# Low weight parts made by ScalarE's negation and an accumulating DMA in place of a subtraction

## The chip, the core and the metric

The kernel runs on one core of a Trainium2 chip. Its metric is the device time of one execution in microseconds (us). Five engines work side by side, each through its own queue in program order: TensorE (PE: matmuls; PEld: weight loads), VectorE (DVE), ScalarE (ACT), GpSimd (POOL) and SyncE (SP, which here only issues DMAs). Waits between engines are semaphores that the framework puts in from the data each instruction reads and writes.

## What is computed

One step of a four-layer decoder trunk over 512 prompt rows and 32 sample rows of width 1024. Each layer is a token mixer and a SwiGLU network, and the layers have a different mixer each: pooling, a Conformer convolution, a chunked gated MLP, a short convolution.

```python
for i in range(DEPTH):                       # 4 layers
    h = _rmsnorm(x, norm_mix[i])
    y, s = mixer[i](h, ...)                  # pool, conv, chunk_gmlp, short_conv
    x = x + y
    x = x + _swiglu(_rmsnorm(x, norm_ffn[i]), ffn_w_in[i], ffn_w_out[i])

def _swiglu(h, w_in, w_out):                 # D_FF = 2816
    gate, up = jnp.split(jnp.einsum('bld,df->blf', h, w_in), 2, axis=-1)
    return jnp.einsum('blf,fd->bld', jax.nn.silu(gate) * up, w_out)
```

All is float32, and nearly all the arithmetic is in the products with the weights.

## The kernel before

**Three matmuls a product.** TensorE takes its operands in a rounded form of float32 (F32R). To keep the precision, every weight and every activation is split into a high part (the value rounded to F32R) and a low part (the value less the high part), and a product is high x high + high x low + low x high, three matmuls into one accumulator. For a weight the high part is a cast on ScalarE (`Load.high`, L159), and the low part a subtraction raw - high (`Load.low`, from L161) on VectorE or GpSimd. All operations of VectorE, GpSimd and TensorE are recorded at L102, the helper that keeps an estimate of each engine's time (`dve.t`, `pool.t`, `pe.t`).

**Loads.** A weight load is 128 partitions by 1024, 768 or 640 columns: `raw_fi`, `hi_fi`, `lo_fi` and so on. The letters say which product it belongs to: fi and fo are the input and output product of the SwiGLU networks, ci and co of the convolution layer, gi and go of the gated layer, si, sb and so of the short convolution. The raw part is fetched by SyncE's queue (L155). There are four raw buffers, five high buffers (AHI + 1) and four low buffers (ALO + 1).

**Halves.** The 544 rows are two halves: A (256 columns) and B (256 + 32). Up to the second layer's network the two halves go through the layers in turn ("one-half" steps), so that each weight is loaded twice; the convolution's taps for one half, a long row of VectorE operations, run as a background job beside the other half's products. From the gated layer's input product on, both halves are worked in one step ("joint"), except for the gated layer's output product, which is done for A and then for B. A one-half step with a 1024-column load is 24 matmuls, a joint one 48. A step of an output product (fo) takes two loads, 768 and 640 columns, and is 33 or 66 matmuls.

**Order of the work.** The program is a list of steps (`Stream`). `Stream.run` goes through it once, and for each step calls `fetch`, which emits the casts up to four loads ahead of the step's first one, and the low parts up to three ahead; then the step's matmuls; then the evacuations of the step before (on VectorE and ScalarE); then background work, as long as `dve.t` is less than a due time that is worked out from `pe.t`. So a load's cast stands on ScalarE's queue ahead of the evacuations of the step before it was fetched. A buffer's next user waits until TensorE has done the step that last read it.

**Who subtracts.** `share` decides. Where it is true (the networks and products with `rel=True`, that is layer 0's network for B, layer 1's for A, the convolution's input product, and the output products for A of the convolution and the gated layer), the subtraction goes to GpSimd unless `pool.t` runs more than LO_LAG ahead of `pe.t`; elsewhere to VectorE. GpSimd has no other large work in those stages, and hardly any later.

Of the kernel before, what the change touches and what calls it, by code (L numbers as in the profile page):

```python
# [8 lines left out]
F32 = mybir.dt.float32  # L9
F32R = mybir.dt.float32r  # L10
I32 = mybir.dt.int32
AF = mybir.ActivationFunctionType
ALU = mybir.AluOpType
PSUM = bass.MemoryType.PSUM

P = 128
# [48 lines left out]
def trunk_kernel(  # L65
# [7 lines left out]
    nc = tc.nc  # L73
# [4 lines left out]
    wp = ctx.enter_context(tc.tile_pool(name="wp", bufs=1))  # L78
# [3 lines left out]
    act = nc.scalar  # L82

    class Timed:
# [3 lines left out]
        def __init__(self, eng, size, per, fixed, least=0.0):  # L88
            self.eng, self.size, self.per, self.fixed, self.t = eng, size, per, fixed, 0.0
            self.least = least  # L90
# [57 lines left out]
    class Load:  # L148
        def __init__(self, src, n, name, share=0):
            self.src, self.n, self.name, self.share = src, n, name, share  # L150
            self.raw = self.hi = self.lo = None

        def dma(self):
            self.raw = wp.tile([P, 1024], F32, tag="raw", name=f"raw_{self.name}", bufs=NRAW)[:, : self.n]
            nc.sync.dma_start(self.raw, self.src)  # L155
# [4 lines left out]

        def low(self):  # L161
            n, raw = self.n, self.raw
            if self.share is True:
                k = 0 if pool.t < pe.t + LO_LAG else n
            else:
                s = (dve.t - pool.t - BIAS + n * dve.per) / (dve.per + pool.per) if self.share else 0
                k = n - min(max(int(s) // 32 * 32, 0), self.share)
            self.lo = wp.tile([P, 1024], F32R, tag="lo", name=f"lo_{self.name}", bufs=ALO + 1)[:, :n]
            if k:
                dve.tensor_sub(self.lo[:, :k], raw[:, :k], self.hi[:, :k].bitcast(F32))  # L170
            if k < n:
                pool.tensor_sub(self.lo[:, k:], raw[:, k:], self.hi[:, k:].bitcast(F32))
# [6 lines left out]
    class Stream:  # L179
        def __init__(self):  # L180
            self.steps, self.loads = [], []
            self.nd = self.nh = self.nl = 0
            self.pending, self.side, self.jobs, self.draining = [], [], [], False
            self.held, self.fill = False, None

        def add(self, loads, mm, evac, flush=False, fill=None):

            for l in loads:
                if l not in self.loads[-6:]:
                    self.loads.append(l)  # L190
            self.steps.append(Step(loads, mm, evac, flush, fill))

        def do(self, fn):
# [85 lines left out]
    S = Stream()  # L279
# [757 lines left out]


    gk = {}

    def gm_consts():
        k = cp.tile([P, PM_COLS], F32, tag="consts", name="gk")
        ws = k[:, :512].rearrange("p (g t) -> p g t", g=NG)
        bs = k[:, 512:1024].rearrange("p (g t) -> p g t", g=NG)
        wss = k[:NS, 1024:1152].rearrange("p (g t) -> p g t", g=NG)
        nc.sync.dma_start(ws, wsT)
        nc.sync.dma_start(wss, wsS)
        nc.sync.dma_start(bs, gm_bs.partition_broadcast(P))

        for g in range(NG):  # L1050
            for w_, n in ((ws, CH), (wss, NS)):
                pool.affine_select(
                    out=w_[:, g, :], in_=w_[:, g, :], pattern=[[1, n]],
                    compare_op=ALU.is_ge, fill=0.0, base=0, channel_multiplier=-1,
                )
        gk.update(ws=ws, bs=bs, wss=wss)
        for nm, src in (("g", gm_g), ("b", gm_b)):
            gk["ln" + nm] = []
            for g in range(NG):
                t = T(f"ln{nm}{g}")  # L1060
                nc.sync.dma_start(t[:, :256], q4(src)[g].partition_broadcast(P)[:, 0, :])
                gk["ln" + nm].append(t)
# [251 lines left out]
    S.run()  # L1314


NRAW, AHI, ALO = 4, 4, 3
FIRST = (
    ("W", (0,)), ("x", (0, 1)), ("w", (0,)), ("W", (1,)), ("x", (2, 3, 4, 5)), ("w", (1,)), ("lo", (0,)),
    ("x", (6, 7)), ("lo", (1, 2, 3, 4, 5, 6, 7)), ("W", (2,)), ("w", (2,)),  # L1320
# [131 lines left out]
```

## Time and profile before

| | |
|---|---|
| median of three runs | 2192.82 us (2192.27 to 2196.62) |
| profiled execution: time, span | 2191.2 us, 2189.3 us |
| TensorE busy | 2156.0 us (98%) |
| VectorE, ScalarE, GpSimd busy | 1298.7, 851.4, 542.7 us |
| moved by SyncE's queue | 279.47 MB in 110376 packets, 42.7% of 16 DMA engines |

"Busy" counts an engine's own instructions, not waiting or issuing. The table of stages in the prediction has, for a stretch of the span, each engine's busy time with its count of instructions in brackets, the clock that was granted to TensorE (1.00 is full), the busy share of the 16 DMA engines and what they moved. A row of waits names who waited, for whom, how many us in total, how often, and the longest. A row of a group has its count, then its busy time and the mean length of one in ns, then the engine's idle time ahead of it and what ended it. A row of DMA issues has the count, the KB of one and the median us from issue to landing. In a row of the timeline stand the start, the length, the engine, the operation, and in brackets the idle time ahead of it.

### The profile page before, as it was taken

Reading aid. Unit: us, or ns where it says so; the run is one execution under the profiler, and the core shown is the slowest. Engines: PE = TensorE matmul, PEld = TensorE weight load, DVE = VectorE, ACT = ScalarE, POOL = GpSimd, SP = SyncE. Lnnn points to the kernel's source line nnn. Section 1 sums busy time; section 2 is a strip of 40 time slices with the busy share of each in tenths; the row PEclk is TensorE's granted clock in tenths of the full one; section 3 lists DMA queues with packets and bytes.
Section 4 is the critical chain, followed back from the end, with each engine's and each line's share of the span. In section 5 each row is a group of like instructions: output and inputs, shape, how many; then the busy total and the mean of one; then the engine's idle time right before and its main releaser. Section 6 shows DMA issues by size and latency. Waiting matters only on the chain.

```text
span 2189.3 us, 41838 instructions
## 1 busy us (share of the span) xinstructions
PE 2156.0 (98%) x17110; PEld 2147.0 (98%) x17110; DVE 1298.7 (59%) x2613; ACT 851.4 (39%) x1372; POOL 542.7 (25%) x378
## 2 busy tenths in 40 slices
PE   9999999999999999999989999999999999999997
PEld 9999999999999999999989999999999999999997
DVE  7867798517999566565587443344555554434444
ACT  5445543545444654444335322232412233222332
POOL 3011787888788910000050000000000000000001
PEclk9999999999999999999999999999999999999998
DMA  8645555556755554545224223322345422232221
GB/s 272 196 144 167 180 183 154 173 160 183 172 164 179 170 191 142 187 146 174 79 91 140 88 70 95 106 85 67 111 81 89 97 87 88 63 102 96 81 74 61
DMA packets 112039, 284.07 MB, mean 130 GB/s; under 512 B 30540, under 2 KB 37800, under 8 KB 111584
## 3 DMA queue, kind: packets, MB, share of 16 engines
q1 hardware_dynamic: 110376, 279.47, 42.7%
q8 instruction: 134, 2.20, 0.4%
q10 hardware_dynamic: 1152, 1.32, 0.2%
q0 software_dynamic: 320, 0.62, 0.1%
q14 instruction: 57, 0.47, 0.1%
HBM read 277.11 MB, written 4.62 MB: 129 GB/s over the span
## 4 chain that ended last, share of the span: by engine, by line
PE 83%; DVE 12%; DMA 2%; ACT 1%; issue 1%; POOL 1%; SPq 0%; DVEq 0%; POOLq 0%; ACTq 0%
PE ps_o L102 22%; PE ps_g L102 20%; PE ps_u L102 20%; DVE ct L102 4%; PE ps_gv L102 3%; PE ps_co L102 2%; PE ps_sc L102 2%; PE ps_sx L102 2%; PE ps_sbg L102 2%; PE ps_so L102 2%; DVE cw L102 1%; DMA raw_fi<-in_w_fin 1%; PE ps_go L102 1%; PE ps_cg L102 1%; DVE vT L102 1%
## 5 line engine op out<-in xcount | busy, mean ns | idle before, releaser
L102 DVE TENSOR_TENSOR lo_fi<-raw_fi,hi_fi 128x1024 fp32r<-128x1024 f32 (+1 forms) x180 | 222.4, 1237 | 332.2 <-issue 258.2
L159 ACT CAST hi_fi<-raw_fi 128x1024 fp32r<-128x1024 f32 x264 | 276.4, 1049 | 346.5 <-PE ps_g L102 111.6
L102 PE MATMUL ps_o<-H_p,hi_fo 128*128 128x288 f32 (+1 forms) x1408 | 351.6, 288 | 1.2 <-ACT H_p L512 1.0
L102 PE MATMUL ps_o<-L_p,hi_fo 128*128 128x288 f32 (+1 forms) x1408 | 351.6, 288 | 0.2
L102 PE MATMUL ps_o<-H_p,lo_fo 128*128 128x288 f32 (+1 forms) x1408 | 351.3, 288 | 0.0
L159 ACT CAST hi_fo<-raw_fo 128x768 fp32r<-128x768 f32 x192 | 149.9, 782 | 287.1 <-PE ps_o L102 154.2
L102 PEld LDWEIGHTS ps_o<-H_p,hi_fo 128*128 128x128 f32 x1408 | 246.4, 188 | 1.6 <-ACT H_p L512 1.6
L102 DVE TENSOR_TENSOR lo_fo<-raw_fo,hi_fo 128x768 fp32r<-128x768 f32 (+1 forms) x128 | 113.5, 890 | 225.4 <-issue 104.8
L102 PEld LDWEIGHTS ps_o<-L_p,hi_fo 128*128 128x128 f32 x1408 | 246.4, 188 | 0.5 <-DVE L_p L102 0.5
L102 PEld LDWEIGHTS ps_o<-H_p,lo_fo 128*128 128x128 f32 x1408 | 246.7, 188 | 0.1
L102 PE MATMUL ps_g<-hH_f,lo_fi 128*128 128x256 f32 (+1 forms) x1040 | 241.8, 288 | 0.8 <-DVE lo_fi L102 0.8
L102 PE MATMUL ps_g<-hH_f,hi_fi 128*128 128x256 f32 (+1 forms) x1040 | 242.2, 288 | 0.1
L102 PE MATMUL ps_u<-hH_f,hi_fi 128*128 128x256 f32 (+1 forms) x1040 | 242.2, 288 | 0.0
L102 PE MATMUL ps_g<-hL_f,hi_fi 128*128 128x256 f32 (+1 forms) x1040 | 241.9, 288 | 0.0
L102 PE MATMUL ps_u<-hL_f,hi_fi 128*128 128x256 f32 (+1 forms) x1040 | 241.8, 287 | 0.0
L102 PE MATMUL ps_u<-hH_f,lo_fi 128*128 128x256 f32 (+1 forms) x1040 | 241.7, 288 | 0.0
L102 POOL TENSOR_TENSOR lo_fi<-raw_fi,hi_fi 128x1024 fp32r<-128x1024 f32 (+1 forms) x86 | 207.6, 2430 | 23.1 <-PE ps_g L102 6.9
L102 DVE SCALAR_TENSOR_TENSOR ct<-ce,colsT,ct 128x256 f32<-128x256 f32 x448 | 182.1, 480 | 0.0
L102 PEld LDWEIGHTS ps_g<-hH_f,lo_fi 128*128 128x128 f32 x1040 | 175.7, 188 | 1.0 <-DVE lo_fi L102 1.0
L102 PEld LDWEIGHTS ps_g<-hH_f,hi_fi 128*128 128x128 f32 x1040 | 176.1, 188 | 0.5 <-ACT hi_fi L159 0.3
L102 PEld LDWEIGHTS ps_u<-hH_f,hi_fi 128*128 128x128 f32 x1040 | 176.0, 188 | 0.1
L102 PEld LDWEIGHTS ps_g<-hL_f,hi_fi 128*128 128x128 f32 x1040 | 175.9, 188 | 0.0
(370 smaller groups left out, 4835.4 us busy)
## 6 DMA issues: line engine op xcount, KB each, us to landing
raw_fi<-in_w_fin SPq DMA_DIRECT2D x264, 512.0 KB, 3.9
raw_fo<-in_w_fout SPq DMA_DIRECT2D x96, 384.0 KB, 3.2
raw_fo<-in_w_fout SPq DMA_DIRECT2D x96, 320.0 KB, 3.0
raw_ci<-in_w_cin SPq DMA_DIRECT2D x32, 512.0 KB, 4.3
raw_co<-in_w_cout SPq DMA_DIRECT2D x16, 512.0 KB, 4.8
raw_gi<-in_w_gin SPq DMA_DIRECT2D x16, 512.0 KB, 3.8
raw_go<-in_w_gout SPq DMA_DIRECT2D x16, 512.0 KB, 3.8
raw_si<-in_w_sin SPq DMA_DIRECT2D x16, 512.0 KB, 3.8
```

What stands on the lines that cost most here:

```text
L102: return fn(*a, **k)
L159: act.copy(self.hi, self.raw)
```

## The change

A load may carry a mark, `sum`. For a marked load, `Load.low` does not subtract: ScalarE writes the negated high part into the low buffer (L167 of the changed kernel), and a DMA from GpSimd's queue reads the weight from HBM a second time and adds it to what lies there (L168). The raw buffer of such a load is then read by the cast alone. The raw DMA itself stays.

The mark is set when a step is added to the list, for loads after the eighth (SUM_FROM): every load whose `share` is false from the gated layer on (`S.joint`), and otherwise every second load. In the one-half stages the second is the "up" one of the two loads of a network's input product, and the 640-column one of an output product. In all 384 loads are marked: 256 of 1024 columns, 96 of 640 and 32 of 768. The gated layer's output product for B, whose steps are one-half, has `share` false, so all its eight loads are marked. ALO goes from 3 to 4: there is a fifth low buffer, and low parts are emitted as far ahead as the casts.

```diff
+            self.sum = False
...
         def low(self):
             n, raw = self.n, self.raw
+            if self.sum:
+                self.lo = wp.tile([P, 1024], F32R, tag="lo", name=f"lo_{self.name}", bufs=ALO + 1)[:, :n]
+                act.activation(self.lo, self.hi.bitcast(F32), AF.Copy, scale=-1.0)
+                nc.gpsimd.dma_start(self.lo, self.src, accum_op=ALU.add)
+                return
             if self.share is True:
...
+            self.joint = False
...
             for l in loads:
                 if l not in self.loads[-6:]:
                     self.loads.append(l)
+                    joint = not l.share and self.joint
+                    l.sum = len(self.loads) > SUM_FROM and (joint or len(self.loads) % 2 == 0)
...
     gk = {}
+    S.joint = True
...
-NRAW, AHI, ALO = 4, 4, 3
+NRAW, AHI, ALO = 4, 4, 4
+SUM_FROM = 8
```

Neither the negation nor the DMA is counted in `dve.t` or `pool.t`. VectorE has 2588 rows of instructions before and 2296 after, ScalarE 1382 and 1766, GpSimd 383 and 675; TensorE and SyncE have the same ones.

On ScalarE's queue, in the output product of layer 0 for half A (`hi_fo0_1_4` is the load of layer 0, second part, output block 4; hH_n1 and sq_n1 are the evacuations). Before:

```order
L420 ACTIVATE sq_n1_0_1_2891<-x0_72 128x256
L159 CAST hi_fo0_1_4_0_17_2897<-raw_fo0_1_4_0_17_2797 128x640
L159 CAST hi_fo0_1_5_0_11_2903<-raw_fo0_1_5_0_11_2842 128x768
L434 ACTIVATE hH_n1_0_2_2943<-x0_72,colsT_74 128x256
L420 ACTIVATE sq_n1_0_2_2945<-x0_72 128x256
L159 CAST hi_fo0_1_5_0_17_2951<-raw_fo0_1_5_0_17_2848 128x640
L159 CAST hi_fo0_1_6_0_11_2957<-raw_fo0_1_6_0_11_2895 128x768
```

Now:

```order
L161 CAST hi_fo0_1_4_0_17_2927<-raw_fo0_1_4_0_17_2826 128x640
L167 ACTIVATE lo_fo0_1_4_0_17_2929<-hi_fo0_1_4_0_17_2927 128x640
L161 CAST hi_fo0_1_5_0_11_2934<-raw_fo0_1_5_0_11_2832 128x768
L444 ACTIVATE hH_n1_0_2_2978<-x0_72,colsT_74 128x256
L430 ACTIVATE sq_n1_0_2_2980<-x0_72 128x256
L161 CAST hi_fo0_1_5_0_17_2982<-raw_fo0_1_5_0_17_2878 128x640
L167 ACTIVATE lo_fo0_1_5_0_17_2984<-hi_fo0_1_5_0_17_2982 128x640
L161 CAST hi_fo0_1_6_0_11_2989<-raw_fo0_1_6_0_11_2884 128x768
L444 ACTIVATE hH_n1_0_3_3033<-x0_72,colsT_74 128x256
```

A negation stands behind each 640-column cast; the 768-column loads of these stages are still subtracted, on VectorE.

On GpSimd's queue, in the input product of layer 0 for half B (cm is an accumulation for the convolution's layer norm). Before:

```order
L102 TENSOR_TENSOR lo_fi0_5_1_0_4126<-raw_fi0_5_1_0_3961,hi_fi0_5_1_0_4086 128x1024
L102 TENSOR_TENSOR cm_0_3747<-cm_0_3747,cc_0_2_3900 128x256
L102 TENSOR_TENSOR lo_fi0_5_1_1_4169<-raw_fi0_5_1_1_4003,hi_fi0_5_1_1_4130 128x1024
L102 TENSOR_TENSOR lo_fi0_6_1_0_4210<-raw_fi0_6_1_0_4044,hi_fi0_6_1_0_4173 128x1024
L102 TENSOR_TENSOR lo_fi0_6_1_1_4250<-raw_fi0_6_1_1_4084,hi_fi0_6_1_1_4214 128x1024
L102 TENSOR_TENSOR lo_fi0_7_1_0_4291<-raw_fi0_7_1_0_4128,hi_fi0_7_1_0_4254 128x1024
```

Now:

```order
L102 TENSOR_TENSOR lo_fi0_5_1_0_4135<-raw_fi0_5_1_0_3968,hi_fi0_5_1_0_4133 128x1024
L168 DMA lo_fi0_5_1_1_4179<-in_w_fin 128x1024
L102 TENSOR_TENSOR cm_0_3794<-cm_0_3794,cc_0_2_3948 128x256
L102 TENSOR_TENSOR lo_fi0_6_1_0_4223<-raw_fi0_6_1_0_4055,hi_fi0_6_1_0_4221 128x1024
L168 DMA lo_fi0_6_1_1_4264<-in_w_fin 128x1024
L102 TENSOR_TENSOR lo_fi0_7_1_0_4305<-raw_fi0_7_1_0_4137,hi_fi0_7_1_0_4303 128x1024
L168 DMA lo_fi0_7_1_1_4346<-in_w_fin 128x1024
```

Every second subtraction has become the issue of a DMA, and each issue waits on this queue for ScalarE's negation, with the next subtraction and the accumulation queued behind it.

## The prediction, made before the changed kernel was run

> **What bounds the kernel now.** I read the page's shares first, then a table of the stages, then TensorE's own waits. The span and TensorE's line of the page:
>
> ```profile
> span 2189.3 us, 41838 instructions
> ...
> PE 2156.0 (98%) x17110; PEld 2147.0 (98%) x17110; DVE 1298.7 (59%) x2613; ACT 851.4 (39%) x1372; POOL 542.7 (25%) x378
> ```
>
> TensorE is busy for 2156.0 of 2189.3 us. The change touches no matmul, so 33.3 us are all that any change off TensorE can win, and part of that lies at the start (the rows of pd and warm below). The profiled execution took 2191.2 us, 1.9 more than its span, and the median of the runs shown is 2192.82, another 1.6 above it. Sums below start from 2191.2 and the 1.6 is added at the end.
>
> The stages (one-half input products, convolution and output products up to 1030, then both halves together; busy times, granted clock, DMA share, GB/s):
>
> ```profile
> core 0: us, PE busy (x) PEld busy (x) DVE busy (x) ACT busy (x) POOL busy (x), PEclk, DMA share, GB/s
> 21.00:238.00 217.00, 215.15 (x1797) 213.60 (x1795) 164.48 (x302) 109.04 (x175) 35.55 (x31) 1.00 0.60 187
> 238.00:295.00 57.00, 55.76 (x457) 55.57 (x458) 46.72 (x118) 28.54 (x37) 47.87 (x36) 1.00 0.53 176
> 295.00:520.00 225.00, 225.00 (x1724) 224.75 (x1724) 136.76 (x312) 104.71 (x168) 184.90 (x106) 1.00 0.54 167
> 520.00:601.00 81.00, 76.63 (x589) 76.07 (x588) 76.34 (x160) 35.12 (x51) 62.13 (x41) 0.98 0.76 176
> 601.00:820.00 219.00, 212.83 (x1730) 210.09 (x1729) 169.08 (x340) 109.81 (x178) 154.64 (x89) 1.00 0.57 176
> 820.00:1050.00 230.00, 230.00 (x1757) 229.78 (x1756) 135.31 (x222) 103.63 (x155) 2.12 (x8) 1.00 0.51 159
> 1050.00:1160.00 110.00, 104.14 (x804) 101.94 (x802) 84.82 (x165) 41.84 (x83) 36.51 (x29) 0.97 0.27 88
> 1160.00:1560.00 400.00, 399.88 (x3198) 399.69 (x3199) 175.87 (x335) 127.47 (x211) 2.65 (x3) 1.00 0.30 93
> ```
>
> Two things are to be seen. TensorE lacks time only in 520 to 820 (10.5 us) and 1050 to 1160 (5.9); from 1160 on, where every load changes, it lacks nothing (0.1 us in 400), so there the change can only cost. And the one-half stages move 159 to 187 GB/s, the joint ones about 93. TensorE's waits, longest first:
>
> ```profile
> PE ps_go L102 <- ACT H_gy L512: 3.5, 1, 3.5
> PE ps_gu L102 <- DVE ce L102: 2.8, 1, 2.8
> PE mix L102 <- DVE vT L102: 2.1, 1, 2.1
> PE ps_g L102 <- POOL lo_fi L102: 1.8, 2, 1.4
> PE pd L102 <- DVE ht L102: 1.6, 1, 1.6
> PE ps_ca L102 <- DVE cc L102: 1.6, 1, 1.6
> PE ps_g L102 <- DVE cc L102: 1.5, 1, 1.5
> PE warm L102 <- DVE ones L102: 1.1, 1, 1.1
> PE ps_o L102 <- ACT H_p L512: 1.0, 1, 1.0
> PE ps_cga L102 <- ACT hH_n L434: 1.0, 1, 1.0
> PE ps_cg L102 <- DVE ct L102: 1.0, 1, 1.0
> ```
>
> Single waits, most of them for VectorE work that is not a low part. Only one of these rows names a low part, 1.8 us. After the three longest that lie inside, the granted clock falls for a while; the 3.4 us behind each:
>
> ```profile
> 573.00:576.40 3.40, 3.39 (x18) 3.40 (x19) 3.37 (x7) 0.99 (x1) 0.00 (x0) 0.59 0.97 298
> 1105.40:1108.80 3.40, 3.40 (x18) 3.40 (x19) 3.33 (x7) 0.00 (x0) 1.80 (x3) 0.60 0.36 123
> 1128.60:1132.00 3.40, 3.22 (x15) 2.84 (x16) 2.73 (x5) 1.36 (x2) 2.20 (x1) 0.70 0.15 58
> ```
>
> The clocks of 0.59, 0.60 and 0.70 cost 0.41, 0.40 and 0.30 of 3.4 us, so 1.4, 1.4 and 1.0. So a long wait costs TensorE half as much again.
>
> **The change, part by part.** The costs of the work that goes and comes, by the groups of the page:
>
> ```profile
> L102 DVE TENSOR_TENSOR lo_fi<-raw_fi,hi_fi 128x1024 fp32r<-128x1024 f32 (+1 forms) x180 | 222.4, 1237 | 332.2 <-issue 258.2
> L159 ACT CAST hi_fi<-raw_fi 128x1024 fp32r<-128x1024 f32 x264 | 276.4, 1049 | 346.5 <-PE ps_g L102 111.6
> ...
> L102 POOL TENSOR_TENSOR lo_fi<-raw_fi,hi_fi 128x1024 fp32r<-128x1024 f32 (+1 forms) x86 | 207.6, 2430 | 23.1 <-PE ps_g L102 6.9
> ```
>
> *Removed.* VectorE loses 292 subtractions of about 1.24 us at 1024 columns, GpSimd 92 of 2.43 us. Where this meets a wait of TensorE:
> GpSimd in 601 to 820 had a subtraction for nearly every load and was late twice; with every second one gone its 154.64 us fall by nearly half, and the 1.8 us go.
> In 1050 to 1160 VectorE loses the 16 of the gated input product and those of its output product; four to six of them, 5 to 7 us, stand ahead of the normalisation and the gating. Against waits of 2.1 (with 1.4 of clock) and 3.5 (with 1.0) I take the first as gone and 2 us of the second, 5.5 in all; the bounds are 0 and 8.0.
> In 520 to 645 the 2.8, 1.6, 1.5 and 1.0 us are waits behind convolution taps and normalisation. By the order of its instructions VectorE does only three low parts shortly before, 3 x 1.24 = 3.7 us, and the code that fills VectorE with taps up to a due time will fill the room again. Of these 6.9 us and the 1.4 of clock behind the 2.8, 8.3 together, I take 3; the bounds are 0 and 8.3.
> Two waits of 1.0 at 238 to 253 I leave, and 0.5 us more for small ones. Sum: 1.8 + 5.5 + 3 + 0.5 = 10.8; all at their upper bounds, 1.8 + 8.0 + 8.3 + 2.0 = 20.1.
>
> *Added on ScalarE.* 384 negations, priced as casts of the same width: 256 of 1.05 us, the rest of 0.71 or 0.84, about 364 us, raising it from 851 to 1215 of 2189. In 601 to 820 (176 GB/s x 219 us are 73 loads of 0.524 MB, half of them 37) it goes from 110 to about 110 + 37 x 1.05 = 149 of 219 us, still a third idle. The negation stands right behind its cast and needs the same release by TensorE, so it adds no new wait on its queue, but the evacuations behind it come up to 1.05 us later. Of that I charge 1 us, at the gating of 1050 to 1160, where TensorE waits for ScalarE; between 0 and 2.
>
> *Buffers.* One more low buffer lets subtraction k run one load earlier, now right behind its cast; VectorE and GpSimd then wait up to 1.05 us for it, in stages where they are not the last. Nothing charged.
>
> *Added DMAs.* 384 of them, 178 MB (256 x 524,288 + 96 x 327,680 + 32 x 393,216 bytes) on top of 279. No accumulating DMA is in the trace, so its price is bounded. What the engines can move at most, from the busiest stretch:
>
> ```profile
> 12.00:16.00 4.00, 4.00 (x38) 4.00 (x37) 3.07 (x7) 4.00 (x13) 4.00 (x6) 1.00 0.99 387
> ```
>
> About 390 to 400 GB/s at a share of 0.99. Let an accumulated byte cost r plain ones. r is at least 1 (it is read from HBM and written like a plain one) and, if reading the source, reading the destination and writing were three separate passes, 3. I take 2, for the added read of the destination. In a one-half stage half of the bytes come again: 187 + r x 93.5 against 400 gives a limit of r = 2.28 in 21 to 238; at 167 GB/s it is 2.79. With r = 2 the first is at 94%, so no stage is bound, but queues are long. The joint stages hold up to 93 x (1 + r) = 400, r = 3.3. One place is over even so: the output product of the gated stage for the second half takes one-half steps with every load accumulated. Eight loads of 0.524 MB need (1 + 2) x 0.524/0.4 = 3.9 us each, against steps of about 3.2 (24 matmuls of 288 columns, where 33 of 256 take 3.88 us, below); 6 us short, of which a prefetch of four loads hides most. I charge 2 there and 2 for long queues in 21 to 820.
>
> By the nearest row alone, the plain load, r would be 1, the first stage at (187 + 93.5)/400 = 70%, and the 4 us would not be charged: 2183. The Trainium skill (Collectives: The Full Stack, section The bandwidth ceiling: the fold count and why AG ≠ RS ≠ AR) speaks against that: an add in the DMA path is dear because it reads two sources, not for the adding, and runs at 32.35 GB/s where a copy has 62.28, a ratio of 1.93; by it the stage is at (187 + 1.93 x 93.5)/400 = 92% and the charge stays. No run so far shows an accumulating DMA.
>
> *Does a low part land in time?* The tightest steady place is the output product of a half. ScalarE there, in order of time:
>
> ```profile
> 216.91 0.84 ACT L159 CAST hi_fo<-raw_fo 128x768 fp32r<-128x768 f32 x1 [0.33 <-ACT hi_fo L159]
> 218.97 0.51 ACT L434 ACTIVATE hH_n<-x,colsT 128x256 fp32r<-128x256 f32 x1 [1.21 <-DVE x L102]
> 219.38 0.40 ACT L420 ACTIVATE sq_n<-x 128x256 f32<-128x256 f32 x1
> 219.69 0.71 ACT L159 CAST hi_fo<-raw_fo 128x640 fp32r<-128x640 f32 x1
> 220.79 0.84 ACT L159 CAST hi_fo<-raw_fo 128x768 fp32r<-128x768 f32 x1 [0.39 <-PE ps_o L102]
> ```
>
> A step takes 220.79 - 216.91 = 3.88 us and one begins at about 220.7. The 640-column piece cast at 219.69 to 220.40 belongs to the step after that, which begins at 224.6, and its low part is read after 20 of 33 matmuls, 2.35 us later: 226.95. So 6.5 us remain for negation, issue and landing. The nearest rows are a plain load of this size, a load from GpSimd's queue, and what such an issue holds GpSimd:
>
> ```profile
> raw_fo<-in_w_fout SPq DMA_DIRECT2D x96, 320.0 KB, 3.0
> ```
>
> ```profile
> stp<-in_st_pool POOLq DMA_DIRECT2D x4, 120.0 KB, 5.9
> ```
>
> ```profile
> L838 POOL DMA_DIRECT2D stp<-in_st_pool x4: 543/543/559, 30.1 to 33.2; - x4
> ```
>
> 0.71 + 0.54 leave 5.2 us for landing. I estimate 3.0 plus 0.8 for reading 320 KB more at 400 GB/s, plus 1 for the queue: 4.8, nearer to the plain load because the 5.9 was taken while much else was in flight. That fits by 0.4 us. The 1024-column loads have four steps of lead, and the joint steps twice the time.
>
> **Sum.** 2191.2 - 10.8 + 1 + 4 = 2185.4, and 1.6 for the median: **2187 us**.
>
> **Rivals.**
> *DMA engines bound (slower).* If r is 3, the one-half stages need (x + 1.5x)/400: 117% of 217 us, 110% of 57, 104% of 225, 110% of 81 and 110% of 219, so 37 + 6 + 9 + 8 + 22 = 82 us more: 2269. It decides from r = 2.28. For it: the share of 0.76 in 520 to 601 and 0.97 at 573, with plain loads alone. Against it: two of the three passes run at once in a plain load.
> *Late low parts in the output products (slower).* If landing takes the 5.9 us of the POOL row, each is 0.7 late; as a late step also gives the next more lead, half of that stays, over 64 one-half steps: 64 x 0.35 = 22, so 2209. It decides from a landing of 5.2.
> *Nothing to win (same).* The taps refill VectorE, the gated stage's waits are on chains that low parts do not delay, and what is won (the 1.8) is lost in queues: 2190 to 2195.
> That low parts are still subtracted is excluded by the order of the instructions.
>
> **Chances.** Forecast 0.45; nothing to win 0.20; engines bound 0.20; late low parts 0.15. About 0.2% (4.4 us) is what a measurement of this kernel can tell from no change. Faster by more 0.45, within 0.20, slower by more 0.35. The range begins at 2176, short of all upper bounds together (2191.2 - 20.1 + 1.6 = 2173), and ends at 2269, r = 3. The forecast's own range is 2176 to 2189.
>
> **What would show it.** Right: the wait for GpSimd's lo_fi gone, those of 1050 to 1160 shorter, clock rows of 1.00 there, accumulating DMAs landing in under 5.2 us in the one-half output products, DMA share below 0.95 in 21 to 238. Wrong: new waits of TensorE for low parts or high parts (hi_fi behind raw_fi, which would be full engines), spread over 21 to 820; or the old waits unchanged.

## The result, and the profile after

The changed kernel takes 2296.95 us (median of four runs, 2294.64 to 2305.21) against 2194.02 of the kernel before on the same chip: a ratio of 1.0475, 95% interval 1.0445 to 1.0505. It is 103 us slower. The prediction was 2187 us, and its range ended at 2269. Two slow executions, one of plain_copy at 5006.40 us and one of the kernel before at 2984.80, count in no ratio, and plain_copy's 2255.60 us below is the median of its other three.

The page after, its span and the busy times:

```profile
span 2297.4 us, 42528 instructions
...
PE 2192.5 (95%) x17110; PEld 2172.8 (95%) x17110; DVE 993.6 (43%) x2321; ACT 1187.9 (52%) x1756; POOL 665.3 (29%) x670
```

VectorE lost 305 us of work (1298.7 before) and ScalarE gained 336 (the prediction had 364). TensorE does the same 17110 matmuls. Its idle time is 2297.4 - 2192.5 = 104.9 us where it was 33.3, so 71.6 more, and its busy time grew by 36.5, since matmuls after a wait run at a lower clock. The two make the 108.1 us between the spans. TensorE's waits, longest first:

```profile
PE ps_u L102 <- DMA lo_fi<-in_w_fin: 24.0, 17, 4.6
PE ps_o L102 <- DMA lo_fo<-in_w_fout: 18.1, 19, 3.0
PE ps_gu L102 <- DMA lo_fi<-in_w_fin: 9.9, 3, 4.1
PE ps_ca L102 <- DMA lo_ci<-in_w_cin: 8.6, 5, 3.5
PE ps_cga L102 <- DMA lo_ci<-in_w_cin: 7.5, 2, 6.3
PE ps_go L102 <- DMA lo_go<-in_w_gout: 5.2, 5, 2.5
...
PE ps_o L102 <- ACT H_p L522: 3.2, 1, 3.2
...
PE ps_co L102 <- DMA lo_co<-in_w_cout: 2.5, 4, 1.0
...
PE ps_gv L102 <- DMA lo_gi<-in_w_gin: 1.8, 1, 1.8
...
PE ps_go L102 <- ACT H_gy L522: 1.0, 1, 1.0
```

Eight rows name an accumulating DMA, 77.6 us together. None names GpSimd's subtractions. The 3.5 us for H_gy has become 1.0, and the 1.8 for GpSimd's lo_fi is gone. By these rows alone one would say that late DMAs are the whole of it. The experiments show otherwise. The stages, cut at the changed kernel's own boundaries:

```profile
22.00:269.00 247.00, 222.68 (x1754) 218.02 (x1752) 131.40 (x266) 134.66 (x207) 55.89 (x64) 0.96 0.83 220
330.00:577.00 247.00, 238.01 (x1799) 236.53 (x1798) 133.84 (x341) 150.28 (x218) 150.31 (x115) 0.99 0.93 238
642.00:884.00 242.00, 223.85 (x1786) 219.52 (x1785) 163.94 (x346) 150.67 (x222) 134.17 (x107) 0.98 0.95 242
884.00:1108.00 224.00, 216.28 (x1599) 214.42 (x1598) 93.54 (x177) 131.48 (x183) 34.63 (x40) 0.98 0.90 231
1290.00:1690.00 400.00, 399.85 (x3192) 399.44 (x3191) 93.56 (x248) 184.54 (x274) 65.82 (x76) 1.00 0.83 178
```

The last two columns are the DMA engines' share and GB/s. The one-half stages with a network stand at 0.83 to 0.95, where they were at 0.51 to 0.60. The last row, network 2 in joint steps with every load marked, lost hardly anything (see the table of stages below). The DMA rows (queue 0 carries the accumulating DMAs, queue 1 SyncE's plain loads; of an issue, the last number is the median landing):

```profile
q0 software_dynamic: 55616, 178.91, 46.9%
q1 hardware_dynamic: 110376, 279.47, 38.4%
...
raw_fi<-in_w_fin SPq DMA_DIRECT2D x264, 512.0 KB, 6.1
lo_fi<-in_w_fin POOLq DMA_DIRECT2D x172, 512.0 KB, 7.5
...
lo_fo<-in_w_fout POOLq DMA_DIRECT2D x96, 320.0 KB, 5.2
```

An accumulated MB took 0.469 x 16 x 2297.4 / 178.91 = 96.4 us of one engine, a plain one 0.384 x 16 x 2297.4 / 279.47 = 50.5. So r is 1.91, next to the 2 that the prediction took. (The Trainium skill, Collectives: The Full Stack, section The bandwidth ceiling: the fold count and why AG ≠ RS ≠ AR, has 1.93, by the bandwidths of its ReduceScatter and AllGather; 1.91 is close to it.) Against the same DMAs as plain copies, in the run plain_copy below, it is less: they took 27.5% of 16 engines over 2259.0 us for the 178.91 MB, or 55.6 us a MB, and 96.4 / 55.6 is 1.73.

Where the time lies, by stage, for the kernels that the argument rests on. Each number is the time from the first matmul of the stage to that of the next, in the profiled execution (late_sub's took 2308.2 us, 14 more than its median, so its column is somewhat too long):

| stage | before | after | alo4 | no_add | late_sub_no_add | late_sub | unread_add |
|---|---|---|---|---|---|---|---|
| layer 0 network A, pooling B | 210.9 | 247.0 | 239.9 | 233.5 | 210.9 | 231.4 | 229.7 |
| convolution input, A | 48.9 | 60.9 | 50.6 | 53.4 | 47.4 | 55.6 | 52.2 |
| network 0 B, convolution output A | 235.1 | 247.2 | 239.5 | 241.0 | 235.6 | 257.4 | 247.6 |
| convolution input, B | 53.5 | 65.0 | 53.9 | 53.0 | 53.0 | 66.7 | 64.7 |
| network 1 A, convolution output B | 228.9 | 242.8 | 231.0 | 220.2 | 221.2 | 255.3 | 249.0 |
| network 1 B | 211.4 | 224.0 | 236.6 | 217.9 | 211.2 | 215.3 | 212.0 |
| gated layer | 172.5 | 181.5 | 186.0 | 170.3 | 171.6 | 184.4 | 173.6 |
| network 2, joint | 397.5 | 399.8 | 410.8 | 398.6 | 398.1 | 398.2 | 407.3 |
| the rest, joint | 609.2 | 607.6 | 610.4 | 608.9 | 609.6 | 614.3 | 611.5 |

(The names are those of the experiments below.)

### The profile page after: what moved, and what is told of

Read it like the earlier page. It is cut to its first block, busy times and chain, and to the rows that moved or that the text cites. A ratio compares the mean times of both kernels' runs of the same rounds, so it can differ in the third digit from the quotient of the medians.

```text
span 2297.4 us, 42528 instructions
## 1 busy us (share of the span) xinstructions
PE 2192.5 (95%) x17110; PEld 2172.8 (95%) x17110; DVE 993.6 (43%) x2321; ACT 1187.9 (52%) x1756; POOL 665.3 (29%) x670
## 3 DMA queue, kind: packets, MB, share of 16 engines
q0 software_dynamic: 55616, 178.91, 46.9%
q1 hardware_dynamic: 110376, 279.47, 38.4%
## 4 chain that ended last, share of the span: by engine, by line
PE 63%; issue 15%; DMA 10%; DVE 5%; POOL 4%; ACT 3%; POOLq 0%; ACTq 0%; DVEq 0%
PE ps_u L102 17%; PE ps_g L102 16%; PE ps_o L102 14%; DMA lo_fi<-in_w_fin 4%; PE ps_gv L102 3%; PE ps_sc L102 2%; PE ps_sx L102 2%; PE ps_sbg L102 2%; PE ps_so L102 2%; DMA lo_ci<-in_w_cin 2%; DMA lo_fo<-in_w_fout 1%; PE ps_gu L102 1%; POOL lo_fi L168 1%; DVE vT L102 1%; DMA raw_fi<-in_w_fin 1%
## 5 line engine op out<-in xcount | busy, mean ns | idle before, releaser
L102 PE MATMUL ps_o<-H_p,lo_fo 128*128 128x288 f32 (+1 forms) x1408 | 355.0, 290 | 18.1 <-DMA lo_fo<-in_w_fout 18.1
L168 POOL DMA_DIRECT2D lo_fi<-in_w_fin x172 | 150.1, 872 | 745.5 <-ACT lo_fi L167 377.2
L168 POOL DMA_DIRECT2D lo_fo<-in_w_fout x128 | 111.5, 871 | 421.4 <-ACT lo_fo L167 326.7
L102 PEld LDWEIGHTS ps_u<-hH_f,lo_fi 128*128 128x128 f32 x1040 | 177.5, 190 | 18.2 <-DMA lo_fi<-in_w_fin 18.1
L167 ACT ACTIVATE lo_fi<-hi_fi 128x1024 fp32r<-128x1024 f32 x172 | 182.4, 1060 | 5.5
L102 PEld LDWEIGHTS ps_u<-hL_f,hi_fi 128*128 128x128 f32 x1040 | 177.9, 190 | 0.0
```

The costliest lines, as they stand in the source:

```text
L102: return fn(*a, **k)
L167: act.activation(self.lo, self.hi.bitcast(F32), AF.Copy, scale=-1.0)
L168: nc.gpsimd.dma_start(self.lo, self.src, accum_op=ALU.add)
```

## The experiments

Each stands with its ratio to the kernel before, measured on the same chip. Diffs of the first four and of late_sub are against the changed kernel.

**Which part of the change costs?** Four kernels: marks on the joint loads alone, on the one-half loads alone, the DMA left out, and a plain copy in its place. (Here Q is the theory that the DMA engines are full, L that low parts land too late for the lead they have.)

```diff
joint_only:
-    l.sum = len(self.loads) > SUM_FROM and (joint or len(self.loads) % 2 == 0)
+    l.sum = len(self.loads) > SUM_FROM and joint
half_only:
+    l.sum = len(self.loads) > SUM_FROM and (not self.joint and len(self.loads) % 2 == 0)
no_add:
-                nc.gpsimd.dma_start(self.lo, self.src, accum_op=ALU.add)
plain_copy:
+                nc.gpsimd.dma_start(self.lo, self.src)
```

> Accumulates only from the gated layer on; the one-half stages subtract as before. Theory Q (the accumulated loads of the one-half stages land late because they share nearly full DMA engines with the raw loads) and theory L (each accumulate simply takes longer from cast to landing than its four steps of lead, however full the engines are) both expect the waits for low parts ahead of 1050 us to vanish, and the time to come back to 2185 to 2200 us: 88 us of the after kernel's 103 lie there; what stays is the gated stage with its 5 us of waits for lo_go. Theory S (the joint stages lose too, through ScalarE or queues that the profile does not show) expects 2210 or more.

> Every second load of the one-half stages is accumulated as in the after kernel, the joint stages subtract on VectorE again. Theories Q and L expect 2285 to 2300 us, within 15 us of after, less the 5 us of waits for lo_go for the second half plus what the gated stage's subtractions cost. Theory S expects less than 2260.

> The marked loads are negated and the accumulating DMA is left out, so their low parts are wrong (the added weight is missing); all else is the after kernel. Theories Q and L expect all waits for low parts gone and the time of the removed work: about 2180 to 2190 us. Theory S (ScalarE's negations, 364 us of them, push the evacuations back) expects it to stay above 2230.

> The same 384 DMAs from GpSimd's queue, but copying instead of adding, so the marked low parts are the whole weight instead of its low part. It halves what an accumulated packet costs the engines (328 ns against 159 for 4096 bytes). Theory Q expects the share of the DMA engines in the one-half stages to fall from about 0.92 to about 0.70, landings of 512 KB to fall from 7.5 to 5 us or less, and 2185 to 2205 us. Theory L, with issue and completion as the long part, expects landings to fall only by the packets' own 1.3 us, to about 6.2, and roughly half of the loss to stay: 2230 to 2260.

Measured: joint_only 2272.13 us, ratio 1.0346 (1.0328 to 1.0364); half_only 2319.22, 1.0559 (1.0538 to 1.058); no_add 2224.62, 1.0129 (1.0112 to 1.0147); plain_copy 2255.60, 1.0253 (1.0221 to 1.0285). None of the four came out as Q expected; plain_copy lies where L expected it, the others in no range of Q or L. The surprise is joint_only. In layer 0's network A it does what the kernel before does, with no DMA added, and takes 241.9 us there where that takes 210.9; network 1 B takes 236.9 for 211.4. What is left of the change in these stages is the fifth low buffer, with subtractions emitted one load earlier. half_only shows the same from the other side: it is 22 us slower than the changed kernel, with 410.9 us in network 2, where its subtractions are back and the changed kernel has 399.8. And no_add is 29 us slower than before with not one byte moved more. Neither Q nor L explains that, so a third theory, C, was formed: a subtraction that stands right behind its own cast ties VectorE and ScalarE into a loop.

**The buffer alone, and the subtractions put back.** The first is the kernel before with one number changed, which sets both the low buffers and how many loads ahead a subtraction is emitted. The other two keep the early negations and DMAs of the changed kernel, but emit the subtractions that are left three loads ahead, as before; the second leaves the DMA out.

```diff
alo4 (against the kernel before):
-NRAW, AHI, ALO = 4, 4, 3
+NRAW, AHI, ALO = 4, 4, 4
late_sub (SUB = 3, low buffers ALO + 2, NBUF 100 for 104):
-            hi, lo = min(cur + 1 + AHI, end), min(cur + 1 + ALO, end)
-            while self.nl < lo or self.nh < hi:
...
+            hi, lo = min(cur + 1 + AHI, end), min(cur + 1 + SUB, end)
+            while self.nh < hi:
+                self.high()
+                if self.loads[self.nh - 1].sum:
+                    self.loads[self.nh - 1].low()
+            while self.nl < lo:
+                if not self.loads[self.nl].sum:
+                    self.loads[self.nl].low()
+                self.nl += 1
late_sub_no_add (against late_sub):
-                nc.gpsimd.dma_start(self.lo, self.src, accum_op=ALU.add)
```

> The kernel before with one change: ALO 4 in place of 3, so every subtraction is emitted one load earlier, right behind its own cast. No negation, no accumulating DMA. Theory C (the subtraction that follows its own cast closes a loop of ScalarE and VectorE: cast, subtraction, evacuations on VectorE, evacuations on ScalarE, next cast): the one-half stages in which VectorE subtracts every load, 21 to 238 and 820 to 1030, lose 15 to 20%, as the run with marks in the joint stages alone did there (a loop of 3.4 us against steps of 2.8): 2255 to 2290, with waits of TensorE for hH_f, H_p and low parts by VectorE. Rival (the buffer is harmless, as the prediction had it; the loss of that run came from its accumulating DMAs): 2190 to 2200.

> The changed kernel with the negations and accumulating DMAs emitted as early as there, but the subtractions that are left emitted three loads ahead, as in the kernel before (one more low buffer, six in all). Theory C: the coupling goes and the waits for the DMAs stay: 30 to 45 us off, 2250 to 2270, with the waits for H_p, hH_f and for VectorE's or GpSimd's low parts gone. Theory Q/L (all of the loss that matters is the DMAs', by full engines or late landing): 2285 or more.

> As late_sub, with the accumulating DMA left out (the negation stays, so the marked low parts are the negated high part and the weight is missing from them). Theory C: nothing is left but what the removed subtractions win, against the negations: 2180 to 2195. Rival (it is ScalarE's negations, not the subtractions' place, that cost the 30 us which the kernel without the addition showed): 2215 to 2225.

Measured: alo4 2285.99, ratio 1.0417 (1.04 to 1.0433); late_sub 2294.52, 1.0435 (1.0402 to 1.0468); late_sub_no_add 2182.83, 0.9944 (0.9929 to 0.9959).

alo4 bears C out: with that one number changed, the kernel before is 4% slower. How, the timeline shows. VectorE in alo4, in layer 0's network A (in brackets the idle time ahead and what ended it):

```profile
68.44 1.22 DVE L102 TENSOR_TENSOR lo_fi<-raw_fi,hi_fi 128x1024 fp32r<-128x1024 f32 x1 [1.42 <-ACT hi_fi L159]
69.59 0.42 DVE L102 TENSOR_TENSOR q<-ps_u,r_f 128x256 f32<-128x256 f32 x1
70.04 0.42 DVE L102 TENSOR_TENSOR q<-q,t 128x256 f32<-128x256 f32 x1
71.88 1.23 DVE L102 TENSOR_TENSOR lo_fi<-raw_fi,hi_fi 128x1024 fp32r<-128x1024 f32 x1 [1.42 <-ACT hi_fi L159]
...
75.20 1.23 DVE L102 TENSOR_TENSOR lo_fi<-raw_fi,hi_fi 128x1024 fp32r<-128x1024 f32 x1 [1.42 <-ACT hi_fi L159]
```

ScalarE in alo4, the same place:

```profile
70.50 0.41 ACT L512 CAST H_p<-q 128x256 fp32r<-128x256 f32 x1 [2.08 <-DVE q L102]
70.81 1.04 ACT L159 CAST hi_fi<-raw_fi 128x1024 fp32r<-128x1024 f32 x1
73.81 0.42 ACT L552 ACTIVATE t<-t 128x256 f32<-128x256 f32 x1 [1.96 <-DVE t L102]
```

VectorE in the kernel before, the same product:

```profile
61.43 1.22 DVE L102 TENSOR_TENSOR lo_fi<-raw_fi,hi_fi 128x1024 fp32r<-128x1024 f32 x1
62.57 0.42 DVE L102 TENSOR_TENSOR L_p<-q,H_p 128x256 fp32r<-128x256 f32 x1
62.90 0.42 DVE L102 TENSOR_TENSOR t<-ps_g,r_f 128x256 f32<-128x256 f32 x1
63.24 1.22 DVE L102 TENSOR_TENSOR lo_fi<-raw_fi,hi_fi 128x1024 fp32r<-128x1024 f32 x1
```

Read them as one chain: subtraction at 68.44, the two rows on q behind it to 70.46, ScalarE's H_p at 70.50 (it waited 2.08 us for q), the next cast at 70.81, the next subtraction at 71.88 (it waited 1.42 for the cast). That is 3.44 us for a load. The next turn, over t, is 71.88 to 75.20, 3.32. TensorE needs 24 x 3.88 / 33 = 2.82 us for the step (33 matmuls took 3.88 in the prediction's rows), so the loop sets the pace. In the kernel before the subtraction takes a cast of a load earlier, nothing in these rows waits, and VectorE can go round in 1.8 us. No engine beside TensorE is full in alo4 (VectorE is busy for 58% of its span, ScalarE for 37%). TensorE's waits in alo4, the longest row and that of the low parts:

```profile
PE ps_o L102 <- ACT H_p L512: 20.9, 8, 3.3
...
PE ps_u L102 <- DVE lo_fi L102: 2.0, 6, 0.3
```

In the input products the loop shows as short waits for a low part, one a step. In the output products it also shows as waits of about 3 us for H_p: at 228.25 us a cast of hi_fo, at 229.09 the subtraction, which waited 1.20 us for it, then the rows on q, at 230.88 H_p, which waited 1.82 us for q, and at 231.34 TensorE, which waited 2.97 us for H_p. In layer 0's network A the output products lose about 20 us of the 29, part of it by the granted clock, which was 0.88 and 0.90 there.

late_sub_no_add shows that with the subtractions back where they were the loop is gone, negations and a sixth low buffer and all, so the order of emission makes it and not the buffer: the 42 us between no_add (2224.62) and it are C's, in the changed kernel's order, and the 384 negations cost nothing that can be seen. It also shows what the freed VectorE wins where nothing else is paid, 13 us. late_sub then says that the DMAs cost far more than C left room for (its time is what Q and L expected): 2294.52 - 2182.83 = 112 us. C and the DMAs do not add up: 42 and 112 are 154, where the changed kernel is 114 us above late_sub_no_add. late_sub runs layer 0's network A faster than the changed kernel (231.4 against 247.0) and network 1 A slower (255.3 against 242.8). In the latter the DMA issues stand earlier on GpSimd's queue than its subtractions, and wait there for negations; TensorE's waits in late_sub name GpSimd's low parts with 7.3 and 4.6 us, where the changed kernel has none. That this order makes the difference is argued, not shown.

**What of the DMAs costs: landing, traffic or GpSimd's queue (H)?** Against late_sub:

```diff
ls_lead6 (NBUF 84; two more raw buffers too):
-NRAW, AHI, ALO = 4, 4, 4
+NRAW, AHI, ALO = 6, 6, 6
ls_fourth:
+    l.sum = len(self.loads) > SUM_FROM and (joint or len(self.loads) % 4 == 0)
ls_copy:
+                nc.gpsimd.dma_start(self.lo, self.src)
ls_lead6_dve (against ls_lead6):
-                k = 0 if pool.t < pe.t + LO_LAG else n
+                k = n
ls_lead6_no_add (against ls_lead6):
-                nc.gpsimd.dma_start(self.lo, self.src, accum_op=ALU.add)
idle_add (three scratch buffers, NBUF 92):
+                nc.gpsimd.dma_start(scraps[-1][:, :n], self.src, accum_op=ALU.add)
unread_add (four low buffers, NBUF 94):
+                self.lo = self.hi
+                scrap = wp.tile([P, 1024], F32R, tag="scrap", name=f"scrap_{self.name}", bufs=5)[:, :n]
+                act.activation(scrap, self.hi.bitcast(F32), AF.Copy, scale=-1.0)
+                nc.gpsimd.dma_start(scrap, self.src, accum_op=ALU.add)
```

> As late_sub, with more lead: casts, negations and accumulating DMAs are emitted six loads ahead in place of four (AHI 6; seven high buffers, eight low ones, six raw ones, paid for with fewer activation buffers, NBUF 84 in place of 100); subtractions stay three ahead. Theory L (the DMAs are late because a low part needs cast 1.05 + negation 1.06 + issue 0.87 + landing 7.5 us, 10.5 in all, out of the 11.2 that four one-half steps of 2.8 us give): with 16.8 us the waits for low parts go, 2190 to 2215. Theory Q (the DMA engines have no room left, shares of 0.90 to 0.97): a longer queue does not help, 2275 or more, with landings longer than before.

> As late_sub, with every fourth load of the one-half stages marked in place of every second; the joint stages as they were. Bytes in a one-half stage in plain ones: 187 x (1 + 0.25 x 2) = 281 GB/s against 374 of late_sub and 400 at most. Theory Q (time is lost where the DMA engines are full): the shares fall to about 0.75 and the loss all but goes, 2190 to 2215. Theory L (each marked load lands too late by its own latency): half the marked loads, so somewhat less than half the 112 us between late_sub and the same without the addition stays, 2225 to 2240.

> As late_sub, with a plain copy in place of the addition (the marked low parts are then the whole weight, not its low part). The same number of DMAs at the same places, but engine time as in ls_fourth: 187 x 1.5 = 281 GB/s. Theory Q: as ls_fourth, 2190 to 2215. Theory L: a copy lands in 5.2 us where an addition takes 7.5, so part of the lateness goes; by the 33 us between the two runs that kept the changed kernel's order (with a copy, without the DMA), 2210 to 2235.

> As ls_lead6 (2236), with the subtractions that are left on GpSimd given to VectorE, so that nothing but small rows stands behind the DMA issues there. Theory H: the waits for GpSimd's low parts (13.7 us in ls_lead6, with the clock behind them about 20) go; VectorE gets about 45 x 1.24 = 57 us more in 300 to 530 and in 600 to 830, where it has 132 and 170 of 230: 2195 to 2220. Rival (VectorE then comes late with the convolution's taps): 2236 or more.

> As ls_lead6 without the accumulating DMAs (the marked low parts are the negated high part): what the longer lead of the casts and the 84 activation buffers cost by themselves. If nothing, as late_sub without the addition: 2180 to 2190. If the early casts on ScalarE's queue or the missing buffers cost: 2200 to 2230, with waits for VectorE's convolution rows (cc, ce) as in ls_lead6.

> As late_sub, with the same accumulating DMAs from the same places of GpSimd's queue, but into three scratch buffers that nothing reads (the marked low parts stay the negated high part; NBUF 92). The traffic is that of late_sub; no low part waits for a landing, and an issue does not wait for the negation. Theory Q (full engines hold back the plain loads, and with them the casts): most of the 112 us stays, 2250 or more, with waits for high parts. Theories L and H (late landings, and issues that hold GpSimd's queue): 2183 to 2205, at shares of DMA near late_sub's.

> As late_sub, with negation and accumulating DMA into a ring of five scratch buffers that nothing reads; the matmuls of a marked load take its high part where the low part would stand (so the low parts of the marked loads are wrong; NBUF 94). Same DMAs, same moments of issue. Theory L (it is TensorE's waits for landings): 2183 to 2200. Theory Q (the traffic delays the raw loads, and through them casts and steps, whoever reads the result): 2250 or more. If both: in between, and the distance to 2183 is Q's part, that to 2294 L's.

| kernel | us | ratio, interval |
|---|---|---|
| ls_lead6 | 2235.72 | 1.0199 (1.0173 to 1.0225) |
| ls_fourth | 2268.72 | 1.037 (1.0322 to 1.0417) |
| ls_copy | 2234.34 | 1.018 (1.0158 to 1.0201) |
| ls_lead6_dve | 2222.84 | 1.0118 (1.0098 to 1.0137) |
| ls_lead6_no_add | 2181.84 | 0.9938 (0.992 to 0.9956) |
| idle_add | 2270.45 | 1.0337 (1.0281 to 1.0394) |
| unread_add | 2275.31 | 1.0361 (1.032 to 1.0401) |

ls_lead6 lies between what L and Q expected. ls_copy, the same DMAs at the same places with plain writes, takes off 60 of the 112 us, the slow end of what L expected; the other 52 stay though nothing is added. ls_fourth missed both, too slow by 29 us and more: half the marks in the one-half stages take off 26. unread_add is the cleanest of them, for only the reader is gone, and 2275.31 - 2182.83 = 92 us are still there. So most of the cost does not need anyone to wait for a landing. (idle_add, in which the DMAs go out with no negation to hold them, has 2270.45, with casts that wait up to 17.5 us for a raw load. Its issues wait for one another instead: for the fi loads alone GpSimd waited 317.0 us until an earlier DMA had landed in the same scratch buffer.) What one sees is that plain loads come late. ScalarE's waits for them in late_sub_no_add:

```profile
ACT hi_fi L161 <- DMA raw_fi<-in_w_fin: 10.7, 7, 4.9
ACT hi_fo L161 <- DMA raw_fo<-in_w_fout: 6.3, 3, 3.0
```

and in unread_add:

```profile
ACT hi_fi L161 <- DMA raw_fi<-in_w_fin: 108.7, 61, 9.3
ACT hi_fo L161 <- DMA raw_fo<-in_w_fout: 34.2, 17, 6.2
```

Eight times the waiting, 142.9 us for 17.0. The rows alone prove little, for the kernel before has such waits as well and is not slowed by them:

```profile
ACT hi_fi L159 <- DMA raw_fi<-in_w_fin: 55.0, 31, 5.1
```

A late raw load makes its cast late, and then what stands behind the cast. One such case is plain in layer 0's network A of unread_add: the cast at 65.13 us had waited 9.34 us for its raw load, and TensorE then waited 3.20 us for that cast.

Why the loads are late has two answers, and no run here separates them. One is the shared engines: the median landing of a raw_fi load is 6.0 us in unread_add and 4.0 in late_sub_no_add. The other is GpSimd's queue. In network 1 A of unread_add SyncE waited 122.9 us (33 times) for GpSimd's subtractions to free a raw buffer before it could fetch the next load, in late_sub_no_add 22.6 us; and TensorE's longest waits in unread_add are 11.3 and 8.9 us for GpSimd's low parts. By the table, 56 of the 91 us between the two profiled executions lie in the four stages in which GpSimd subtracts, 19 in layer 0's network A. A high share alone does not cost the time: network 1 B of unread_add, where GpSimd subtracts nothing, stands at a share of 0.93 and takes 212.0 us for 211.2. The remaining 19 us (late_sub less unread_add; by the intervals of the two ratios, 16 with about 11 either way) are what waiting for the landings adds.

A longer lead, with six raw buffers in place of four, takes away 59 us (late_sub to ls_lead6), and costs nothing by itself (ls_lead6_no_add, as expected). How much of the 59 is due to the lead and how much to the raw buffers is not shown. TensorE's waits for lo_fi by DMA shrink from 22.0 to 2.5 us. ls_lead6_dve then removes the waits for GpSimd's subtractions, 13.7 us, and 13 us of time, a little less than H expected. Network 0 B gains (240.2 to 236.4) and so does the convolution's input product for B (63.2 to 55.5), but network 1 A does not (243.5 to 244.2, with a single wait of 8.3 us for ScalarE there in its place). With no subtraction left on GpSimd and the long lead, the DMAs still cost 2222.84 - 2181.84 = 41 us.

**Versions that might win.**

```diff
joint_alo3 (ALO 3; against the changed kernel):
+    l.sum = len(self.loads) > SUM_FROM and joint and l.name[:2] != "go"
ls_lead6_few and, with k = n as above, ls_lead6_dve_few:
+    l.sum = len(self.loads) > SUM_FROM and (joint and l.name[:2] == 'gi' or not joint and len(self.loads) % 4 == 0)
gated_few (against late_sub; self.gated counts the gi loads):
+    l.sum = joint and l.name[:2] == "gi" and self.gated > 4
```

> The part of the change that TensorE could have used: only loads of the joint steps are marked, without the gated layer's output product (whose steps for half B are one-half), and ALO is 3 as before. Theory C with Q/L: the one-half stages are those of the kernel before, the joint steps are long enough for a landing of 8.8 us (8 us a step of two loads and three loads ahead, so 12 less a cast): 2185 to 2195, at most some single waits of lo_gi at the first gated steps; a gain of up to 2.1 + 1.4 us at the gated layer's start is possible. Rival (the accumulating DMAs hurt also in the joint stages, by landing late at three loads' lead): 2215 or more.

> The version that the runs so far point to: as ls_lead6, with marks only on every fourth load of the one-half stages and on the gated layer's input product; no marks after it, where TensorE lacked nothing before. Theory L with C: no low part late, and part of the 13 us that late_sub without the addition won: 2178 to 2192. Theory Q or a cost of the smaller NBUF: 2195 or more.

> As ls_lead6_dve, with marks only on every fourth load of the one-half stages and on the gated layer's input product. By L and H together: 2180 to 2200, the version that could beat both. If VectorE becomes late with three of four subtractions and the taps on it: 2230 or more.

> As late_sub, with marks on 12 loads only: the gated layer's input product without its first four loads, at a DMA share of about 0.3. By what the runs showed (traffic costs where the engines are near full, subtractions in step with their casts cost, three loads of lead are too few at the first gated load): no low part late, and the 2.1 us wait for vT and part of the 3.5 us for H_gy gone with their clock, against new waits for gt of 2 to 5 us as in joint_alo3: 0 to 5 us less than before, 2190 to 2195. Rival (the landing is late even there): 2197 or more, with a wait for lo_gi.

Measured: joint_alo3 2206.89, ratio 1.0055 (1.004 to 1.007); ls_lead6_few 2267.12, 1.0332 (1.0304 to 1.0359); ls_lead6_dve_few 2232.87, 1.0157 (1.0129 to 1.0186); gated_few 2196.3, 1.0002 (0.9991 to 1.0013). None beats the kernel before; joint_alo3 lies between its two ranges, gated_few is just above its own, and ls_lead6_few lies with its slower theory. joint_alo3 is level with it up to the gated layer (213.4, 48.8, 235.0, 53.6, 229.1 and 211.5 us) and loses 8.8 there, by two new waits:

```profile
PE ps_gv L102 <- DVE gt L102: 4.9, 2, 2.7
PE ps_gv L102 <- DMA lo_gi<-in_w_gin: 4.5, 1, 4.5
```

gated_few, which leaves the first four loads alone, has no wait for lo_gi and is no different from before: the waits for vT and H_gy shrink (the first is gone, the second 2.2), and 4.4 us for gt take their place. The two kernels with few marks were expected to be the best, and each is slower than the one with more marks that it was made from (2267 against 2236, 2233 against 2223). In ls_lead6_dve_few it is the case that its expectation names last: VectorE is late with the taps. GpSimd waited 8.95 us for VectorE's cc, TensorE 11.9 us for GpSimd's cm and 7.5 for what follows it, and the granted clock was 0.50 for 34.1 us from 787 us on; network 1 A takes 262.3 us for 244.2. TensorE's longest row there is still a DMA's, 13.4 us for lo_fi. In ls_lead6_few TensorE's longest row is 14.3 us for GpSimd's lo_fo; why that kernel is 31 us slower than ls_lead6 is not settled.

## Why the prediction was wrong

**The work removed and the negations: right in size.** The prediction had -10.8 and +1. late_sub_no_add, which has these two alone, is 0.9944 of before, so 12 us less. The place was not right, so the agreement of the sums is in part luck. The gated layer, booked with 5.5 us, gave 0.9 (172.5 to 171.6), with 2.2 us of new waits for gt and 2.6 left for H_gy; network 1 A, the GpSimd stage with the convolution's taps, gave 7.7 (228.9 to 221.2), where the 1.8 and part of the 3 us stood. (In ls_lead6_dve the gated layer does take 165.4 us for 172.5.)

**"Buffers. ... Nothing charged."** This is the step that failed in kind. It named the wait (up to 1.05 us for the cast) and set it aside, since VectorE is not the last engine. But VectorE's subtraction waits for ScalarE, ScalarE's evacuation for VectorE's, and the next cast stands behind that evacuation: a closed loop of 3.4 us needs no full engine. By itself the changed number costs 4.2%, and in the changed kernel, where half of the subtractions are gone, 42 us.

**"With r = 2 the first is at 94%, so no stage is bound, but queues are long ... I charge 2 there and 2".** r was nearly right, 1.91, and the charge of 4 us was too small by far. With C taken off, the DMAs cost 112 us; in the changed kernel's order, 2296.95 - 2224.62 = 72. The step took an average share below one for room, and priced neither late plain loads nor the subtractions that stand behind the DMA issues on GpSimd's queue. The rival "DMA engines bound" came nearest on time (2269), but by luck: r stayed below its point of 2.28, and 42 us of the loss are C's. In unread_add plain loads come late at shares of 0.86 to 0.95 with nobody waiting for the accumulated ones, and network 1 B loses 0.8 us at 0.93.

**Landing.** The estimate for 320 KB was 4.8 us against a limit of 5.2; the median is 5.2. TensorE's waits for lo_fo are 18.1 us, and the rival had charged 22. What the text left out is the 1024-column loads, "four steps of lead": cast 1.05, negation 1.06, issue 0.87 and landing 7.5 are 10.5 of the 11.3 us that four steps of 2.82 give, so 0.8 us of room, and these loads have the longest waits of the page.

```profile
L167 ACT ACTIVATE lo_fi<-hi_fi 128x1024 fp32r<-128x1024 f32 x172 | 182.4, 1060 | 5.5
...
L168 POOL DMA_DIRECT2D lo_fi<-in_w_fin x172 | 150.1, 872 | 745.5 <-ACT lo_fi L167 377.2
```

**Clock.** The text had that a long wait costs half as much again, and charged none, as it expected no new waits. It holds: 36.5 us more busy time on 71.6 more idle.

**The joint stages** lose 2.3 us in network 2 and nothing after, as their limit of r = 3.3 said. In the gated layer's output product, charged with 2, TensorE waits 5.2 us for lo_go, and that layer takes 181.5 us for 172.5. What the prediction lists as a sign of being wrong, new waits of TensorE for low parts spread over 21 to 820, is what came.

Open is how the 92 us that the unread DMAs cost split between the shared engines and the order of GpSimd's queue, and why marking a quarter of the loads costs more than its bytes.

## What to carry to other kernels

A producer and a consumer on two in-order queues can need a lag between them: here a consumer emitted one load earlier lost the lag and closed a loop through both queues, though neither engine was full. An average share of the DMA engines says little either way: at 0.93 one stage here lost 0.8 us, at 0.95 another 28. Ask which loads come late and which queue frees their buffers, and add the whole chain from cast to landing up against the lead. Waits that name one transfer in the profile may be the visible end of another cause: leave the reader out, and see what stays.

## What was not expected of the hardware

The clock's answer to a wait is uneven. In the kernel before, waits of 2.1 to 3.5 us were followed by about 3.4 us at 0.6 to 0.7. In no_add two waits of 2.76 and 4.00 us lie 5.3 us apart, at 99.6 and 104.95, and this follows (stretch, TensorE busy and granted clock among the columns):

```profile
100.00:110.00 10.00, 5.95 (x24) 5.29 (x24) 6.26 (x14) 4.85 (x9) 0.00 (x0) 0.50 0.57 168
110.00:120.00 10.00, 10.00 (x45) 9.69 (x44) 0.92 (x2) 0.93 (x3) 0.00 (x0) 0.50 0.05 21
120.00:130.00 10.00, 10.00 (x68) 9.73 (x67) 2.96 (x6) 3.55 (x7) 0.00 (x0) 0.82 0.12 33
```

TensorE is busy all the time from 110 on and stays at half clock to about 124, close to 20 us. The Trainium skill (TensorE: Matmul & The Clock Gate, section Part 1: The HAM clock gate) has the full clock back after about 3.4 us of sustained work; this stretch does not agree with it, the rows of the kernel before do. Half clock lasts 3.4 to 13.7 us nearly everywhere in these traces. Three of the four longer stretches (23.9 us here, 20.5 in unread_add, 27.3 in plain_copy) lie at the same place, where groups of small pd matmuls, 128 columns wide, stand between those of ps_o; the fourth is the 34.1 us of ls_lead6_dve_few. What makes the difference is open. Half clock for 23.9 us costs 12 us, so a part of the 42 us of C, and of the 92 of the unread DMAs, hangs on where a wait fell.
